# The first weight tile of a windowed matmul: two 1 MB halves on one hardware queue, or one half and two quarters spread over two queues

## The chip, the cores and the metric

The kernel runs on one core of a Trainium2 chip. The metric is the device time of one execution in microseconds (us).

## The reference

```python
B, S, D, W = 4, 4096, 4096, 64
for b in range(B):
    o = int(offsets[b])
    results.append(x[b, o:o+W] @ w)      # w is 4096 x 4096, fp32
```

Four windows of 64 rows each are multiplied by one matrix of 64 MB. Nearly all bytes that the kernel moves are `w`, and each is read once.

## The kernel before

The four windows fill two groups of 128 rows (`G = 2`). `w` is cut into 32 k tiles of 128 rows. GpSimd's queue, which can cast while it copies, loads them as fp16 in blocks of up to four k tiles (8 MB read). GpSimd's first packets come late, so the first k tile is loaded ahead of them, as fp32, by the hardware queue of the sync engine (SP), into a tile that is free until later (`acc[1]`), and the scalar engine (ACT) casts it:

```python
    w0_32 = acc[1]
    nc.sync.dma_start(out=w0_32[:, :NG], in_=w[0:P, :NG])          # NG = 2048: 128 rows of 8 KB
    nc.scalar.dma_start(out=off_t[:], in_=offsets[None, :])
    nc.sync.dma_start(out=w0_32[:, NG:], in_=w[0:P, NG:])
    nc.scalar.copy(out=w_one[0][:, :NG], in_=w0_32[:, :NG])
    nc.scalar.copy(out=w_one[0][:, NG:], in_=w0_32[:, NG:])
    ...
    nc.gpsimd.dma_start(out=w_one[1][:], in_=w[P : 2 * P, :])      # second k tile, cast on the way
    ...                                                            # x, at addresses read from off_t
    for k0, r in blocks[2:]:                                       # the weight blocks, 3 buffers
        ...
        nc.gpsimd.dma_start(out=t[:, base : base + r * N], in_=w[k0 * P : (k0 + r) * P, :].rearrange(...))
```

x is transposed by matmuls as soon as it has landed; then come the first two k tiles and the blocks.

Of the kernel before, what the change touches and what calls it, by code (L numbers as in the profile page):

```python
# [10 lines left out]
def kernel(  # L11
# [7 lines left out]
    nc = tc.nc  # L19
# [4 lines left out]
    _, N = w.shape  # L24
    WIN = out.shape[1]
    P = 128
    NT = 512
    NG = N // 2
# [32 lines left out]
    ctx.enter_context(tc.manual_schedule())  # L61

    w0_32 = acc[1]
    nc.sync.dma_start(out=w0_32[:, :NG], in_=w[0:P, :NG])
    nc.scalar.dma_start(out=off_t[:], in_=offsets[None, :])
    nc.sync.dma_start(out=w0_32[:, NG:], in_=w[0:P, NG:])
    nc.scalar.copy(out=w_one[0][:, :NG], in_=w0_32[:, :NG])  # L67
    nc.scalar.copy(out=w_one[0][:, NG:], in_=w0_32[:, NG:])  # L68
# [4 lines left out]
    for b in range(B):  # L73
# [9 lines left out]
            out=x16[g][m * WIN : (m + 1) * WIN, :],  # L83
            in_=x[b][bass.ds(o, WIN), :],
# [8 lines left out]
    for k0, r in blocks[2:]:  # L93
        if free < r:
# [5 lines left out]
            out=t[:, base : base + r * N],  # L100
            in_=w[k0 * P : (k0 + r) * P, :].rearrange("(p r) n -> p (r n)", r=r),
# [13 lines left out]
    for ng, st in zip(order, (steps, fine_steps)):  # L115
        for ki, n, c0, c1 in st:
            wd = c1 - c0
            nc.gpsimd.dma_start(  # L118
                out=t[:, pos : pos + n * wd].rearrange("p (t n) -> p t n", t=n),
                in_=w[ki * P : (ki + n) * P, ng * NG + c0 : ng * NG + c1].rearrange(  # L120
                    "(t p) n -> p t n", p=P
                ),
# [14 lines left out]
    for g in range(G):  # L137
        for t in range(4):
            for i in range(8):
                nc.tensor.matmul(  # L140
                    out=pairs[t][:, i * P : (i + 1) * P],
# [126 lines left out]
```

## Time and profile before

| | before |
|---|---|
| time, median of 6 runs | 182.14 us (181.95 to 182.30) |
| span of the profiled run | 180.1 us |
| busy share of PE / DVE / ACT | 71% / 46% / 9% |
| read from HBM, written | 71.3 MB, 4.2 MB |

The busy shares say little here: no compute engine is full, while the DMA engines are. The windows of four single microseconds of the kernel before. Columns: the stretch and its length, busy time of PE, PE's weight loads, DVE, ACT and POOL (with numbers of instructions), granted clock, mean busy share of the 16 DMA engines, GB/s written. The last two count a packet wholly in the microsecond in which it starts, so the share can exceed 1.

```profile
2.00:3.00 1.00, 0.00 (x0) 0.00 (x0) 0.00 (x0) 0.70 (x1) 0.55 (x3) 1.00 0.88 205
3.00:4.00 1.00, 0.00 (x0) 0.00 (x0) 0.00 (x0) 0.00 (x0) 0.46 (x1) 1.00 0.91 369
4.00:5.00 1.00, 0.00 (x0) 0.00 (x0) 0.00 (x0) 0.00 (x0) 0.59 (x2) 1.00 1.01 426
5.00:6.00 1.00, 0.00 (x0) 0.00 (x0) 0.00 (x0) 0.20 (x1) 0.53 (x2) 1.00 1.16 360
```

(From 5 us on part of the traffic is cast from 4 bytes to 2, so that the column of bytes written falls.)

### The profile page before, as it was taken

The page shows a single profiled execution, that of the slowest core. Times are in us where ns is not written, and L with a number is a line of the kernel's source. Part 1 is how long each engine was busy: PE and PEld are TensorE (multiplying, and loading weights), DVE is VectorE, ACT ScalarE, POOL GpSimd, SP SyncE. Part 2 cuts the span into 40 slices and gives each one's busy share as a digit, 9 for nine tenths or more (in the row PEclk, how much of TensorE's full clock was granted, in tenths as well). Part 3 has the DMA queues.
Part 4 walks back from the last instruction along what each step waited for, and adds up shares of the span by engine and source line. Part 5 has one row for each costly group of instructions (what it writes and reads, how often), then busy time and mean ns, then how long its engine had stood idle before and what let it go on. Part 6 is the DMA issues. An engine that isn't in the chain of part 4 may idle for free.

```text
span 180.1 us, 1403 instructions
## 1 busy us (share of the span) xinstructions
PE 128.2 (71%) x576; PEld 57.3 (32%) x576; DVE 82.2 (46%) x68; ACT 16.9 (9%) x15; POOL 12.7 (7%) x27
## 2 busy tenths in 40 slices
PE   0000789104999499938996599949999999999910
PEld 0000764001344134413442134414444444443400
DVE  0000566200276427642566036733778975407560
ACT  2422346200000000000000000000000004004000
POOL 4600000000000100010001000020007100000200
PEclk9999999855599969996999569987999999999995
DMA  5999979999998899999989999999999999999996
GB/s 187 313 260 213 286 160 211 236 233 226 233 233 175 182 233 233 236 218 233 204 175 218 233 233 220 222 193 202 229 206 215 198 211 213 214 214 207 338 412 241
DMA packets 4151, 40.97 MB, mean 227 GB/s; under 512 B 434, under 2 KB 434, under 8 KB 2226
## 3 DMA queue, kind: packets, MB, share of 16 engines
q0 software_dynamic: 3280, 36.70, 93.5%
q1 hardware_dynamic: 576, 3.15, 4.6%
q10 hardware_dynamic: 290, 1.05, 1.5%
q8 instruction: 4, 0.07, 0.1%
q14 instruction: 1, 0.01, 0.0%
HBM read 71.30 MB, written 4.19 MB: 419 GB/s over the span
## 4 chain that ended last, share of the span: by engine, by line
DMA 43%; PE 43%; issue 4%; DVE 2%; another core or an unknown queue 1%; POOLq 1%; DVEq 1%; POOL 1%
DMA wc<-in_w_dram 43%; PE banks L154 43%; DVE acc L164 2%; DVEq L263 1%; POOLq L75 1%; POOL xrow L82 0%; POOL identity masks.py:197 0%; POOLq L82 0%; POOL w L71 0%; POOLq masks.py:199 0%; DVEq L164 0%; POOLq L252 0%
## 5 line engine op out<-in xcount | busy, mean ns | idle before, releaser
L154 PE MATMUL banks<-wc,xT 128*128 128x512 f16 x480 | 115.8, 405 | 23.6 <-DMA wc<-in_w_dram 23.3
L164 DVE TENSOR_TENSOR acc<-acc,banks 128x1024 f32<-128x1024 f32 x56 | 67.9, 1221 | 69.0 <-PE banks L154 68.4
L154 PEld LDWEIGHTS <-xT 128*128 128x128 f16 x512 | 52.3, 103 | 93.9 <-DMA wc<-in_w_dram 26.4
L140 PE MATMUL banks<-identity,xrow 128*128 128x128 f16 x64 | 5.3, 261 | 19.9 <-DMA xrow<-in_x_dram 19.9
L209 ACT COPY tmp<-banks 128x1024 f32<-128x1024 f32 x4 | 3.9, 1016 | 128.2 <-PE banks L154 128.2
L149 DVE CAST xT<-banks 128x1024 f16<-128x1024 f32 x4 | 4.8, 1222 | 21.5 <-PE banks L140 21.5
L99 POOL DMA_DIRECT2D wc<-in_w_dram x8 | 4.3, 539 | 108.1 <-PE banks L154 108.1
L140 PEld LDWEIGHTS <-xrow 128*128 128x128 f16 x64 | 5.1, 127 | 20.0 <-issue 20.0
L154 PE MATMUL banks<-w,xT 128*128 128x512 f16 x32 | 7.1, 379 | 0.0
L182 DVE COPY acc<-banks 128x1024 f32<-128x1024 f32 x4 | 4.9, 1225 | 1.6 <-PE banks L154 1.6
L118 POOL DMA_DIRECT2D wc<-in_w_dram x6 | 3.9, 674 | 17.1 <-PE banks L154 17.1
L213 DVE TENSOR_TENSOR acc<-acc,tmp 128x1024 f32<-128x1024 f32 x4 | 4.7, 1218 | 0.0
L151 ACT CAST xT<-banks 128x1024 f16<-128x1024 f32 x4 | 4.0, 1014 | 7.9 <-PE banks L140 7.9
L184 ACT COPY acc<-banks 128x1024 f32<-128x1024 f32 x4 | 4.0, 1012 | 3.0 <-PE banks L154 3.0
L200 POOL DMA_DIRECT2D out_dram<-acc x2 | 1.1, 537 | 27.2 <-DVE acc L213 27.2
L68 ACT CAST w<-acc 128x2048 f16<-128x2048 f32 x1 | 1.9, 1898 | 4.8 <-DMA acc<-in_w_dram 4.8
L82 POOL DMA_DIRECT2D xrow<-in_x_dram x4 | 2.1, 524 | 2.1 <-issue 2.1
L67 ACT CAST w<-acc 128x2048 f16<-128x2048 f32 x1 | 1.9, 1898 | 3.1 <-DMA acc<-in_w_dram 3.1
L67 ACT ACT_TABLE_LOAD x1 | 1.3, 1283 | 1.4 <-PEq L252 1.4
L71 POOL DMA_DIRECT2D w<-in_w_dram x1 | 0.7, 660 | 0.8 <-POOLq L252 0.8
masks.py:199 POOL TENSOR_SCALAR_AFFINE_SELECT identity<-identity 128x128 f16<-128x128 f16 x1 | 0.3, 287 | 0.1
masks.py:197 POOL MEMSET identity<- 128x128 f16 x1 | 0.2, 223 | 0.0
(4 smaller groups left out, 0.4 us busy)
## 6 DMA issues: line engine op xcount, KB each, us to landing
wc<-in_w_dram POOLq DMA_DIRECT2D x5, 4096.0 KB, 42.1
wc<-in_w_dram POOLq DMA_DIRECT2D x4, 1024.0 KB, 24.5
wc<-in_w_dram POOLq DMA_DIRECT2D x1, 3072.0 KB, 37.1
acc<-in_w_dram SPq DMA_DIRECT2D x2, 1024.0 KB, 8.1
xrow<-in_x_dram POOLq DMA_DIRECT2D x4, 512.0 KB, 14.4
wc<-in_w_dram POOLq DMA_DIRECT2D x1, 2048.0 KB, 26.4
out_dram<-acc POOLq DMA_DIRECT2D x2, 1024.0 KB, 5.6
w<-in_w_dram POOLq DMA_DIRECT2D x1, 1024.0 KB, 11.8
```

What stands on the lines that cost most here:

```text
L67: nc.scalar.copy(out=w_one[0][:, :NG], in_=w0_32[:, :NG])
L99: nc.gpsimd.dma_start(out=t[:, base : base + r * N], in_=w[k0 * P : (k0 + r) * P, :].rearrange("(p r) n -> p (r n)", r=r),)
L118: nc.gpsimd.dma_start(out=t[:, pos : pos + n * wd].rearrange("p (t n) -> p t n", t=n), in_=w[ki * P : (ki + n) * P, ng * NG + c0 : ng * NG ...
L140: nc.tensor.matmul(out=pairs[t][:, i * P : (i + 1) * P], lhsT=x_cols(g, 8 * t + i), rhs=identity[:], start=True, stop=True,)
L149: nc.vector.tensor_copy(out=dst, in_=pairs[t][:])
L151: nc.scalar.copy(out=dst, in_=pairs[t][:])
L154: nc.tensor.matmul(out=banks(bank), lhsT=xT[g][:, kt * P : (kt + 1) * P], rhs=rhs, start=start, stop=stop,)
L164: nc.vector.tensor_add(out=dst, in0=dst, in1=banks(bank, n))
L182: nc.vector.tensor_copy(out=dst, in_=banks(b0, 2))
L184: nc.scalar.copy(out=dst, in_=banks(b0, 2))
L209: nc.scalar.copy(out=tmp[g][:], in_=banks(4 * g + 2, 2))
L213: nc.vector.tensor_add(out=dst, in0=dst, in1=tmp[g][:])
```

## The change

Its intent is to get the first half of the tile in sooner, by loading it as two quarters, one on each hardware queue:

```diff
     w0_32 = acc[1]
-    nc.sync.dma_start(out=w0_32[:, :NG], in_=w[0:P, :NG])
+    Q = N // 4
+    nc.sync.dma_start(out=w0_32[:, :Q], in_=w[0:P, :Q])
     nc.scalar.dma_start(out=off_t[:], in_=offsets[None, :])
+    nc.scalar.dma_start(out=w0_32[:, Q:NG], in_=w[0:P, Q:NG])
     nc.sync.dma_start(out=w0_32[:, NG:], in_=w[0:P, NG:])
```

## The prediction

> **What bounds the kernel now.** I read the page first, then the chain of waits in order of time, the matmuls' timeline, the start's timeline, and the windows of the first microseconds. The page's slices say which resource is full, and the chain says where it sets the end:
>
> ```profile
> PE   0000789104999499938996599949999999999910
> ACT  2422346200000000000000000000000004004000
> PEclk9999999855599969996999569987999999999995
> DMA  5999979999998899999989999999999999999996
> ...
> DMA wc<-in_w_dram 43%; PE banks L154 43%; DVE acc L164 2%; DVEq L263 1%; POOLq L75 1%; POOL xrow L82 0%; POOL identity masks.py:197 0%; POOLq L82 0%; POOL w L71 0%; POOLq masks.py:199 0%; DVEq L164 0%; POOLq L252 0%
> ```
>
> The reader is to see that the DMA engines are about full in nearly every slice from the second on, that the matrix engine is not, and that neither the first k tile's load (acc<-in_w_dram) nor its casts on ACT stand in the chain. The matmuls' timeline shows how the two resources divide the span:
>
> ```profile
> 43.07 16.75 PE L154 MATMUL banks<-wc,xT 128*128 128x512 f16 x64 [10.79 <-DMA wc<-in_w_dram]
> 62.34 15.66 PE L154 MATMUL banks<-wc,xT 128*128 128x512 f16 x64 [2.52 <-DMA wc<-in_w_dram]
> 81.76 15.67 PE L154 MATMUL banks<-wc,xT 128*128 128x512 f16 x64 [3.75 <-DMA wc<-in_w_dram]
> 101.14 16.73 PE L154 MATMUL banks<-wc,xT 128*128 128x512 f16 x64 [3.71 <-DMA wc<-in_w_dram]
> 120.44 49.93 PE L154 MATMUL banks<-wc,xT 128*128 128x512 f16 x218 [2.57 <-DMA wc<-in_w_dram]
> ```
>
> Blocks of 8 MB of weights arrive every 19.3 us ((120.44-43.07)/4), about 433 GB/s of reading; PE needs 15.7 to 16.8 us for each and waits 2.5 to 3.8 us. After 120.44 us it no longer waits for long: 218 matmuls in one piece, then the last additions and stores. So the end is "landing of the fifth block" plus a fixed PE and store tail, and the landing is the sum of all DMA work queued before it, as the engines never run dry. Only what adds to that sum, or removes idle time from it, can move the end. The start, which the change touches:
>
> ```profile
> 0.86 0.52 ACTq L65 DMA_DIRECT2D off_t<-in_offsets_dram  x1
> 0.87 0.38 SPq L64 DMA_DIRECT2D acc<-in_w_dram  x1
> 1.30 0.42 SPq L66 DMA_DIRECT2D acc<-in_w_dram  x1
> 1.39 0.66 POOL L71 DMA_DIRECT2D w<-in_w_dram  x1 [0.81 <-POOLq L252]
> 1.42 1.28 ACT L67 ACT_TABLE_LOAD   x1 [1.42 <-PEq L252]
> ...
> 5.80 1.90 ACT L67 CAST w<-acc 128x2048 f16<-128x2048 f32 x1 [3.10 <-DMA acc<-in_w_dram]
> ...
> 12.53 1.90 ACT L68 CAST w<-acc 128x2048 f16<-128x2048 f32 x1 [4.83 <-DMA acc<-in_w_dram]
> ...
> 18.31 3.40 PE L140 MATMUL banks<-identity,xrow 128*128 128x128 f16 x32 [18.31 <-DMA xrow<-in_x_dram]
> ...
> 23.29 1.95 PE L140 MATMUL banks<-identity,xrow 128*128 128x128 f16 x32 [1.58 <-DMA xrow<-in_x_dram]
> ...
> 25.21 5.12 PE L154 MATMUL banks<-w,xT 128*128 128x512 f16 x23
> ```
>
> The first k tile is cast by 14.43 us, and its first matmul runs at 25.21, after both transposes that wait for x. That is 10.8 us of slack. Even the x path has slack: the first two k tiles are done some 33 us into the span, and PE then idles 10.79 us until the first block lands at 43.03.
>
> **What the Trainium skill says.** "DMA: Bandwidth & Descriptors", section "Issuing engines are not separate DMA queues": DMAs of the sync, scalar and GpSimd engines run on the same 16 DMA engines and interleave, and issuing from several saves only issue time. The trace agrees: once the GpSimd queue's packets begin, about 5.25 us into the span, single-packet records of the sync queue (8 KB, 0.322 us) alternate with its own (0.624 us each), while the DMA share stays at 0.95 to 1.16. The same page, section "Queues, rings and completion order", says a DMA is split over k of at most 16 rings, and "Why a DMA increments its semaphore by 16 and not by 1" that a 128-partition tile takes all 16. So a quarter spreads as a half does, 8 rows per engine; the trace has 128 packets and 16 semaphore packets for each half. The latter section also says that only the full count means the data has landed, so a cast that reads both quarters must wait for two full counts. The present trace has no two-queue load to test that on.
>
> **The change part by part.** Bytes do not change: 2 MB of fp32 weights, no compute instruction added or removed.
>
> 1. *Packets.* Before: 128 rows of 8 KB for the first half, 8 per engine, 0.309 us each in the packet records once the stream runs: 8 x 0.309 = 2.47 us. After: 16 rows of 4 KB per engine. The only 4 KB packets on these two queues in the trace are the final stores, median 0.159 us; taking that for loads too is my estimate. 16 x 0.159 = 2.54 us. Added: +0.07 us of DMA time, and one more semaphore packet per engine at 0.009 us. Sum +0.08 us, in a stream that has no idle time, so on the path.
>
> 2. *Issue.* SP issues the same number of DMAs at the same times. ACT issues one more behind the offsets: from about 1.4 us, some 0.4 to 0.5 us long (the row of L66, and of L65). The offsets' DMA still goes first, so x is issued as before. Nothing here is on the path.
>
> 3. *Landing of the first half.* SP's first packets begin about 0.8 us after its issue (1.68 us); ACT's should begin near 2.2 us. Its 8 packets per engine then alternate with the sync queue's, which has 1 to 3 packets' lead and, its quarter done, puts 1 to 3 rows of 8 KB of the other half between. So the quarter on ACT ends 0.3 to 0.9 us (1 to 3 x 0.309) later than the half did: the first half lands a little **later**, not earlier.
>
> 4. *A new wait.* In the built instruction stream the ACT table load, which waited for no DMA, now carries the wait for ACT's quarter, ahead of the cast that waits for SP's. So its 1.28 us no longer hide under the transfer: the first cast should start near 5.80 + 0.3 to 0.9 + 1.3 = 7.4 to 8.0 us. It ends before 10 us, ahead of the second cast, whose half lands at about the same time as before (12 us, perhaps up to 1 us sooner, as fewer rows are left to alternate with GpSimd's). Of the 10.8 us of slack nothing near all is used: 0 us.
>
> 5. *Everything behind.* w1, x and the weight blocks are issued from the same GpSimd stream in the same order. With the same bytes ahead of them they land where they did, plus 0.08 us.
>
> Sum: 182.15 + 0.08 = 182.2 us.
>
> **Rivals.**
>
> *A faster ramp.* The first packet of each engine took 0.725 us (median of the first 16 records) and the second 0.361, against 0.309 later: some 0.45 us of the DMA engines' time is lost at the start. If a second queue, or smaller rows, filled that hole, the whole stream and with it the end would move forward by up to 0.4 us: 181.8. For it: the stream is on the path, so every tenth counts in full. Against it: ACT's packets come 0.5 us after SP's, when the hole is mostly over, and may have a slow first packet of their own. I give it about one chance in four to win 0.2 us or more.
>
> *4 KB rows cost more than I take.* At 0.20 us per row it would be 16 x 0.20 - 2.47 = +0.73 us: 182.9. Against it: the stores' 0.159 us, with no load at that size to confirm.
>
> *ACT becomes the wait.* If the late table load and cast held the first matmuls, one would see PE wait for ACT at 25 us. It would need ACT to lose over 10 us; and even then the 10.79 us of idle PE before 43.07 lies behind. No effect on the end.
>
> *The PE clock.* Half-clock stretches come and go (the PEclk row), and after 120.44 us PE has little slack. A 3.4 us stretch at half clock moved into that tail would cost about 1.7 us. Against it: the three runs of before agree within 0.16 us, and a shift of 0.1 us in the stream hardly changes PE's load.
>
> **Range and chances.** The centre is the sum, 182.2. The low side is the ramp in full plus scatter of some 0.2 us, 181.6; the high side is most of the costlier rows, 182.8. Two per cent are 3.6 us: no term above is half of that except the clock's, so within 2% gets 0.98 and the two sides 0.01 each.
>
> **What would show it right or wrong.** Right: two DMAs of 512 KB and one of 1024 KB for acc among the DMA issues; the first cast at 7.4 to 8.0 us with the table load just before it; the second cast at 11.5 to 12.8; transposes still from 18.3 and 23.3 us; blocks landing at 43.1, 62.4, ... 120.5; 4 KB load packets near 0.16 us. The ramp rival is shown if all block landings come 0.2 to 0.4 us sooner, the row rival if they come 0.3 us or more later. Wrong altogether if PE comes to wait for ACT before the first two k tiles, if x lands much later, or if the half-clock stretches fall otherwise after 120 us.

## The result, and the profile after

| | before | changed |
|---|---|---|
| median of 6 runs | 182.14 us | 182.98 us |
| lowest, highest | 181.95, 182.30 | 182.85, 183.08 |

The ratio is 1.0046 (95% interval 1.0033 to 1.0059). Ratios are computed as the mean time of one kernel's runs over that of the other's of the same rounds, so they are not quite the ratio of the medians quoted here. The change is a small loss of 0.84 us, clear of noise, within 2%, and above the predicted range, which ended at 182.8.

From the page of the changed kernel, the DMA row of the 40 slices and the chain of waits by line:

```profile
DMA  5999999999999999999999999989999999999996
...
DMA wc<-in_w_dram 43%; PE banks L156 42%; DVE acc L166 2%; DMA off_t<-in_offsets_dram 1%; POOLq L77 1%; DVEq L265 1%; POOL xrow L84 0%; POOLq L84 0%; DVEq L166 0%
```

As before, the stream is full from the second slice on and the chain alternates between weights and matmuls. New is an entry for `off_t`, the offsets: a suspect, tested below. The matmuls' timeline of the changed kernel:

```profile
44.13 16.83 PE L156 MATMUL banks<-wc,xT 128*128 128x512 f16 x64 [11.03 <-DMA wc<-in_w_dram]
63.46 15.67 PE L156 MATMUL banks<-wc,xT 128*128 128x512 f16 x64 [2.50 <-DMA wc<-in_w_dram]
...
121.43 51.27 PE L156 MATMUL banks<-wc,xT 128*128 128x512 f16 x224 [2.45 <-DMA wc<-in_w_dram]
```

The first block lands 44.13 - 43.07 = 1.06 us later, the fifth 121.43 - 120.44 = 0.99 us later, and the span is 0.9 us longer (181.0 against 180.1). So the whole loss is there before the first block is used, and nothing is added or won back in the next 77 us. The start of the changed kernel's timeline:

```profile
0.87 0.52 ACTq L66 DMA_DIRECT2D off_t<-in_offsets_dram  x1
0.87 0.38 SPq L65 DMA_DIRECT2D acc<-in_w_dram  x1
1.30 0.43 SPq L68 DMA_DIRECT2D acc<-in_w_dram  x1
...
1.42 0.38 ACTq L67 DMA_DIRECT2D acc<-in_w_dram  x1
...
13.04 1.28 ACT L69 ACT_TABLE_LOAD   x1 [13.04 <-DMA acc<-in_w_dram]
14.34 1.90 ACT L69 CAST w<-acc 128x2048 f16<-128x2048 f32 x1
16.14 1.89 ACT L70 CAST w<-acc 128x2048 f16<-128x2048 f32 x1
...
26.04 4.26 PE L156 MATMUL banks<-w,xT 128*128 128x512 f16 x19
```

The first half is complete at 13 us instead of 5.8, because the quarter on ACT's queue lands last of all. That is spectacular and costs nothing: the casts end at 18.03 us, and their first matmul runs at 26.04, behind the transposes of x. What does cost is in the windows of the changed kernel:

```profile
2.00:3.00 1.00, 0.00 (x0) 0.00 (x0) 0.00 (x0) 0.00 (x0) 0.56 (x3) 1.00 0.87 213
3.00:4.00 1.00, 0.00 (x0) 0.00 (x0) 0.00 (x0) 0.00 (x0) 0.00 (x0) 1.00 0.83 217
4.00:5.00 1.00, 0.00 (x0) 0.00 (x0) 0.00 (x0) 0.00 (x0) 0.53 (x1) 1.00 0.99 352
5.00:6.00 1.00, 0.00 (x0) 0.00 (x0) 0.00 (x0) 0.00 (x0) 0.53 (x1) 1.00 1.06 418
```

The second of these lines is the finding: 217 GB/s where the kernel before moves 369, at nearly the same busy share (0.83 against 0.91); spread over the packets' durations, 222 against 361. Full rate comes at 5 us, one microsecond later.

The trace also records single packets, and they were counted directly; these counts are used below. Up to 6 us into the span 1408 KB had been read before and 1165 KB after; up to 12 us, 3959 and 3717 KB. The missing 243 KB are 0.57 us at 427 GB/s. I call a packet slow when it took over 1.3 times the median of its size, and at least 60 ns more. Before, 21 of 256 rows of the first k tile were slow, most of them the first or second row of a DMA engine (up to 1.27 us instead of 0.309). After, 48 of the 128 rows of the quarter that opens the stream were slow (up to 1.06 us instead of 0.159), up to 4.6 us into the span; and from 2.0 to 2.75 us only 10.0 of the 16 engines had a packet in flight on average, against 14.5 before. (A single such count decides little: x3, a run below that loses nothing, has 11.1.)

Slow rows are only half of it. Per DMA engine, the delay splits into the time that the first k tile's packets took, and the time without a packet in flight between 1.88 and 5.2 us. The sum agrees within 0.04 us with how much later the mean engine reaches the first 8 MB block. One profile each, in us against the kernel before; the runs are explained below. Differences under 0.2 us mean little here: x3 sums to +0.16 and loses no time.

| run | packets | no packet in flight | later at the first block, mean engine |
|---|---|---|---|
| changed kernel | +0.31 | +0.28 | +0.56 |
| e1_rows_only | +0.08 | +0.33 | +0.39 |
| y1_one_queue_same_order | +0.43 | +0.21 | +0.61 |
| x2_quarters_last | +0.28 | 0.00 | +0.24 |
| e2_queue_only | +0.15 | -0.05 | +0.08 |
| y4_all_quarters | +0.59 | +0.27 | +0.86 |

Following the DMA engines to their first packets of the first 8 MB block, the mean start moved from 22.33 to 22.89 us and the slowest from 22.59 to 23.64. A block has landed only when all engines have delivered their rows, so the spread counts as well as the mean: the mean engine finishes the first block 0.56 us later (41.70 and 42.26 us), the last one 1.12 us later (42.69 and 43.81). That one engine trails the last but one by 0.80 us before and 0.87 after, so it alone sets the landing.

**Two levels.** Later runs showed that nearly every kernel here has a second level some 0.5 to 1.2 us above its first: of 11 runs of the kernel before in one batch, nine lay at 181.8 to 182.1 and two at 182.8. Profiled runs on the upper level show a lower granted clock in the stretch of back-to-back matmuls at the end. Here the same window for the changed kernel (lower level), for the run with whole rows (upper level) and for the changed kernel run again (upper level); the third figure from the right is the clock:

```profile
120.40:172.00 51.60, 50.31 (x222) 22.12 (x223) 30.20 (x26) 3.85 (x4) 4.99 (x8) 0.97 1.01 221
```

```profile
120.40:172.00 51.60, 50.86 (x221) 22.17 (x222) 29.92 (x25) 3.85 (x4) 4.99 (x8) 0.95 1.01 219
```

```profile
120.40:172.00 51.60, 50.13 (x216) 21.82 (x217) 28.87 (x25) 3.85 (x4) 5.00 (x8) 0.93 0.99 212
```

All 19 profiles follow this: 0.93 to 0.95 in the five on the upper level (and in y3, whose six runs spread too far to be sorted), 0.97 to 1.00 in the other thirteen; and where the last 224 matmuls run in one piece they take 52.1 to 52.4 us on the upper level and 51.2 to 51.3 on the lower. That is a correlation of the right size; no run changed the clock to test it. To keep the draw out of the comparisons I quote, besides the median and the ratio over all runs, the median of the runs on a kernel's lower level. The grouping is mine, and an intermediate run now and then could be sorted either way. The kernel before is at 182.0 to 182.1 in that reading in every later batch.

### The profile page after: what moved, and what is told of

Read it like the earlier page. It is cut to its first block, busy times and chain, and to the rows that moved or that the text cites. A ratio compares the mean times of both kernels' runs of the same rounds, so it can differ in the third digit from the quotient of the medians.

```text
span 181.0 us, 1405 instructions
## 1 busy us (share of the span) xinstructions
PE 128.6 (71%) x576; PEld 57.3 (32%) x576; DVE 82.2 (45%) x68; ACT 16.8 (9%) x15; POOL 12.7 (7%) x27
## 4 chain that ended last, share of the span: by engine, by line
DMA 45%; PE 42%; issue 4%; DVE 2%; another core or an unknown queue 1%; POOLq 1%; DVEq 1%; POOL 0%
DMA wc<-in_w_dram 43%; PE banks L156 42%; DVE acc L166 2%; DMA off_t<-in_offsets_dram 1%; POOLq L77 1%; DVEq L265 1%; POOL xrow L84 0%; POOLq L84 0%; DVEq L166 0%
## 6 DMA issues: line engine op xcount, KB each, us to landing
acc<-in_w_dram SPq DMA_DIRECT2D x1, 1024.0 KB, 10.8
w<-in_w_dram POOLq DMA_DIRECT2D x1, 1024.0 KB, 12.8
```

## The experiments

Three theories stood at first. ROWS: the short rows are to blame. QUEUE: the second hardware queue is. OFFSETS: the offsets' packet, at 2.61 us instead of 1.75 in the profiled run, delayed x.

| run | what opens the stream, and what follows | median, us | lower level (runs on it) | ratio to before |
|---|---|---|---|---|
| changed kernel | 4 KB quarter, half, quarter on ACT | 182.98 | 182.98 (6 of 6) | 1.0046 |
| e1_rows_only | quarter, quarter, half, all on SP | 182.64 | 182.62 (5 of 6) | 1.0035 |
| e2_queue_only | half on SP, half on ACT | 182.12 | 182.07 (5 of 6) | 1.0005 |
| e3_offsets_first | as changed, offsets first on SP | 182.52 | 182.52 (5 of 6) | 1.0029 |
| e4_whole_rows | one transfer, 16 KB rows | 182.49 | 182.04 (3 of 6) | 1.0011 |
| x1_after_again | as changed | 183.39 | 182.91 (3 of 6) | 1.0065 |
| x2_quarters_last | half, then the two quarters | 182.22 | 182.22 (6 of 6) | 1.0003 |
| x3_late_offsets | half, offsets, half on SP | 182.04 | 182.03 (5 of 6) | 1.0002 |
| x4_eighths | four 2 KB pieces, half | 184.46 | 184.46 (4 of 4) | 1.0127 |
| y1_one_queue_same_order | quarter, half, quarter on SP | 182.93 | 182.91 (5 of 6) | 1.0050 |
| y2_half_on_scalar | two quarters on SP, half on ACT | 183.53 | 182.75 (1 of 6) | 1.0071 |
| y4_all_quarters | four quarters on SP | 183.74 | 183.73 (5 of 6) | 1.0096 |
| z4_two_short_row_transfers | 1 MB transfers of 4 KB rows | 184.54 | 184.48 (3 of 5) | 1.0149 |
| z5_quarter_then_rest | quarter, then 12 KB rows | 182.83 | 182.75 (4 of 6) | 1.0052 |

All runs gave correct results. Four more runs (y3, z1, z2, z3) stand with their times in the section on the opening.

### Row length or second queue: e1_rows_only, e2_queue_only

```diff
-    nc.scalar.dma_start(out=w0_32[:, Q:NG], in_=w[0:P, Q:NG])
+    nc.sync.dma_start(out=w0_32[:, Q:NG], in_=w[0:P, Q:NG])
```

> Both quarters of 4 KB rows on the sync queue, then the other half; the scalar queue carries the offsets alone. Theory ROWS (4 KB rows make the start of the stream slower, whichever queue they are on): as slow as the changed kernel, 182.8 to 183.2 us. Theory QUEUE (the second hardware queue, with its late start and its mixing, delays some DMA engines): back at the kernel before, 182.0 to 182.3. Theory OFFSETS (the offsets' packet, 0.9 us later in the changed kernel, delays x and with it the end): follows the offsets' packet, 182.2 if it is back at 1.75 us, 183.0 if it is at 2.6 us.

```diff
 # from the kernel before
-    nc.sync.dma_start(out=w0_32[:, NG:], in_=w[0:P, NG:])
+    nc.scalar.dma_start(out=w0_32[:, NG:], in_=w[0:P, NG:])
```

> 8 KB rows throughout, as before, but the second half on the scalar queue behind the offsets. Theory ROWS: as the kernel before, 182.0 to 182.3 us. Theory QUEUE: slower by half of the loss or all of it, 182.6 to 183.0. Theory OFFSETS: as the kernel before if the offsets' packet comes at 1.75 us as there.

With the second queue alone the time is that of the kernel before (182.07, ratio 1.0005). With the cut alone it is 182.62, and the offsets' packet is at 1.75 us again, so that OFFSETS fails here too. The third and fourth microsecond show why. First the windows of e1_rows_only, then those of e2_queue_only:

```profile
2.00:3.00 1.00, 0.00 (x0) 0.00 (x0) 0.00 (x0) 0.00 (x0) 0.56 (x3) 1.00 0.81 209
3.00:4.00 1.00, 0.00 (x0) 0.00 (x0) 0.00 (x0) 0.00 (x0) 0.47 (x1) 1.00 0.85 238
```

```profile
2.00:3.00 1.00, 0.00 (x0) 0.00 (x0) 0.00 (x0) 1.00 (x1) 0.56 (x3) 1.00 0.87 172
3.00:4.00 1.00, 0.00 (x0) 0.00 (x0) 0.00 (x0) 0.10 (x1) 0.46 (x1) 1.00 0.91 344
```

With the 4 KB quarter at the opening the rate is 238 GB/s in the fourth microsecond, little above the 217 of the changed kernel; with the 8 KB half it rises to 344, second queue or not. So the cut carries most of the loss. But e1 loses 0.55 us and the changed kernel 0.85; 0.3 us were unexplained.

### The offsets: e3_offsets_first, x1_after_again, x3_late_offsets

```diff
 # e3, from the changed kernel
+    nc.sync.dma_start(out=off_t[:], in_=offsets[None, :])
     nc.sync.dma_start(out=w0_32[:, :Q], in_=w[0:P, :Q])
-    nc.scalar.dma_start(out=off_t[:], in_=offsets[None, :])
```

> The changed kernel, with the offsets' transfer issued first on the sync queue, ahead of that queue's quarter. Theory OFFSETS: the offsets' packet and the issue of x are back at their early times and the time falls to about 182.2 us. Theories ROWS and QUEUE: it stays at 182.8 to 183.2, although x is issued 0.6 us sooner.

x1_after_again is the changed kernel unaltered.

> The changed kernel unaltered, once more, to see whether its offsets' packet at 2.6 us and its slowest DMA engine (1.05 us behind the kernel before's at the first 8 MB block) are its own or a draw. Theory ROWS (4 KB rows cost 0.5 us wherever they open the stream; the rest of the 0.85 us is the late offsets' packet or scatter): the loss on the first block is 0.5 to 1.1 us, the time 182.5 to 183.0. Theory ORDER (the offsets' transfer behind a 4 KB quarter adds the other 0.3 us each time): offsets' packet again at 2.6 us and the time at 182.9 to 183.1.

```diff
 # x3, from the kernel before
-    nc.scalar.dma_start(out=off_t[:], in_=offsets[None, :])
+    nc.sync.dma_start(out=off_t[:], in_=offsets[None, :])
```

> The kernel before's two halves of 8 KB rows on the sync queue, with the offsets' transfer put between them on that queue, so that it lands later than in the changed kernel and x is issued later. Theory ROWS: no change, 182.0 to 182.3 us, as x waits behind the second k tile in its queue anyway. Theory OFFSETS: slower by 0.3 us or more, 182.4 to 183.2.

x3 put the offsets' packet at 4.96 us, far later than the changed kernel did, and the time is 182.03: no cost. x1 drew an early packet (1.76 us) and is as slow as ever, 182.91 on its lower level, with 58 slow 4 KB rows and the slowest DMA engine at 23.64 us, as in the first profile. So the late packet in the first profile was a draw, and the entry for `off_t` in the chain is a wait that costs nothing. OFFSETS and its variant ORDER are out. e3 alone would have misled: it gained 0.46 us, but it also put the two quarters one behind the other ahead of the half, as e1 does, and has e1's time.

### Position and dose: x2_quarters_last, x4_eighths, e4_whole_rows, y4_all_quarters

```diff
 # x2: the changed kernel's transfers and queues, the half first
+    nc.sync.dma_start(out=w0_32[:, NG:], in_=w[0:P, NG:])
     nc.scalar.dma_start(out=off_t[:], in_=offsets[None, :])
     nc.sync.dma_start(out=w0_32[:, :Q], in_=w[0:P, :Q])
     nc.scalar.dma_start(out=w0_32[:, Q:NG], in_=w[0:P, Q:NG])
-    nc.sync.dma_start(out=w0_32[:, NG:], in_=w[0:P, NG:])
```

> The same three transfers on the same queues, but the 8 KB half opens the stream and the two quarters follow. Theory COLD START (only the first 2 us of the stream are slow per packet, so that small rows cost there alone): as the kernel before, 182.0 to 182.3 us, with hardly any slow 4 KB packet. Rival (4 KB rows cost the same anywhere, or the third transfer does): 182.5 to 183.0.

```diff
 # x4: E = N // 8, offsets first, then
+    for i in range(4):
+        nc.sync.dma_start(out=w0_32[:, i * E : (i + 1) * E], in_=w[0:P, i * E : (i + 1) * E])
     nc.sync.dma_start(out=w0_32[:, NG:], in_=w[0:P, NG:])
```

> The dose doubled: the first half as four pieces of 2 KB rows, all on the sync queue, then the other half in 8 KB rows; offsets first. Theory COLD START: the first piece moves half as many bytes per slow packet, so the loss grows from the 0.5 us of rows-only to 0.7 to 1.3 us: 182.8 to 183.4. Theory that the loss is a fixed cost of a third transfer or a draw: 182.5 to 182.7.

```diff
 # e4: offsets, then
+    nc.sync.dma_start(out=w0_32[:, :], in_=w[0:P, :])
```

> The whole first k tile as one transfer of 128 rows of 16 KB on the sync queue: the row size changed the other way. Theory ROWS: at the kernel before or faster, 181.6 to 182.2 us, with less time lost per DMA engine before the first 8 MB block. Theories QUEUE and OFFSETS: the kernel before's time, 182.0 to 182.3.

```diff
 # y4: first quarter, offsets, then
+    for i in range(1, 4):
+        nc.sync.dma_start(out=w0_32[:, i * Q : (i + 1) * Q], in_=w[0:P, i * Q : (i + 1) * Q])
```

> All four quarters in 4 KB rows, one after the other on the sync queue. Theory COLD START (only the rows that open the stream cost): as rows-only, 182.5 to 182.7 us in the lower level. Theory that each 4 KB row costs alike, wherever it stands: twice the loss of rows-only, 183.0 to 183.2.

x2 is the cleanest run. The same three transfers, on the same two queues, cost about 0.15 us (ratio 1.0003, not clear of noise) instead of 0.85 when the half goes first; only 7 of its 256 rows of 4 KB are slow. Its windows of the same two microseconds are those of a good start:

```profile
2.00:3.00 1.00, 0.00 (x0) 0.00 (x0) 0.00 (x0) 0.00 (x0) 0.55 (x3) 1.00 0.86 188
3.00:4.00 1.00, 0.00 (x0) 0.00 (x0) 0.00 (x0) 0.00 (x0) 0.46 (x1) 1.00 0.87 328
```

The dose works in one direction only. Shorter rows cost more, and more than I expected: 2 KB rows lose 2.3 us where I had written 0.7 to 1.3. Longer rows (e4) win nothing; on the lower level they are at 182.04. And the opening is not all: y4 has e1's opening and the same 0.82 to 0.83 MB read by 5 us, but ends 1.1 us later than e1. Two parts of that can be read from the records. First, its engines reach the first 8 MB block 0.47 us later than e1's (0.86 against 0.39 above), all of it packet time, against the expectation of COLD START that later 4 KB rows are free. Of this, 0.18 us is their price beside GpSimd's packets: on SP's queue a 4 KB row takes 0.172 us there and an 8 KB row 0.322, so two short rows cost 0.022 us more than a long one, and y4 has eight such pairs per engine more than e1. Second, 0.42 us are lost after the last store and have nothing to do with rows. At its end SP checks a row of semaphores one after the other, and in y4 the wait for the last store comes first instead of near the end. SP's wait for the stores in e1, then in y4 (us in total, number of waits, the longest):

```profile
SPq L265 <- DMA out_dram<-acc: 4.0, 4, 1.2
```

```profile
SPq L265 <- DMA out_dram<-acc: 4.7, 1, 4.7
```

In y4 the whole wait falls on one instruction, and seven more, some 0.06 us each, run after it. From the last packet of the stores to the end of the span it is 1.70 us in y4, 1.71 in z1 and 1.64 in x4, and 1.26 to 1.29 in the other 16 profiles. These three kernels have the most transfers ahead of the stream; what orders the waits was not looked into. So about 0.4 us of the losses of y4, z1 and x4 come from the end of the program.

### The missing 0.3 us: y1_one_queue_same_order, y2_half_on_scalar, z5_quarter_then_rest

```diff
 # y1, from the changed kernel
+    nc.sync.dma_start(out=w0_32[:, NG:], in_=w[0:P, NG:])
+    nc.sync.dma_start(out=w0_32[:, Q:NG], in_=w[0:P, Q:NG])
-    nc.scalar.dma_start(out=w0_32[:, Q:NG], in_=w[0:P, Q:NG])
-    nc.sync.dma_start(out=w0_32[:, NG:], in_=w[0:P, NG:])
```

> Rows-only cost 0.5 us (182.6), the changed kernel costs 0.85 (182.9 in the lower of the two levels that every kernel shows). Here all three transfers are on the sync queue, in the order in which the changed kernel's packets started: first quarter, 8 KB half, second quarter. Theory SECOND QUEUE (the other 0.3 us comes from two hardware queues at once): 182.5 to 182.7 in the lower level. Theory ORDER OF SIZES (it comes from the half following the first quarter directly): 182.8 to 183.0.

```diff
 # y2, from the changed kernel: the second and third weight transfers change queues
+    nc.sync.dma_start(out=w0_32[:, Q:NG], in_=w[0:P, Q:NG])
+    nc.scalar.dma_start(out=w0_32[:, NG:], in_=w[0:P, NG:])
-    nc.scalar.dma_start(out=w0_32[:, Q:NG], in_=w[0:P, Q:NG])
-    nc.sync.dma_start(out=w0_32[:, NG:], in_=w[0:P, NG:])
```

> Both quarters on the sync queue, the 8 KB half on the scalar queue: two hardware queues as in the changed kernel, but the large rows on the other. Theory SECOND QUEUE: 182.8 to 183.0 us in the lower level. Theory ORDER OF SIZES: 182.5 to 182.7, if the second quarter's packets start before the half's; 182.9 if not.

```diff
 # z5: first quarter, offsets, then
+    nc.sync.dma_start(out=w0_32[:, Q:], in_=w[0:P, Q:])
```

> A first quarter of 4 KB rows, then all the rest as one transfer of 12 KB rows, both on the sync queue. Both theories: slower than before. SMALL OPENING TRANSFER and ORDER OF SIZES: as the changed kernel, 182.8 to 183.0 in the lower level, as large rows follow the quarter directly. If only the count of 4 KB rows mattered (half as many as in rows-only): 182.3.

y1 uses one queue only and has the changed kernel's whole loss: 182.91 on the lower level, ratio 1.0050. That settles that no second queue is needed for it. What y1 shares with the changed kernel, and e1 and e3 do not, is the half directly behind the first quarter: in the trace of the changed kernel the half's first row starts at 4.01 us, while ACT's quarter, issued 0.12 us after the half, starts only at 4.68. The fifth microsecond of y1 moves 340 GB/s (352 in the changed kernel, 393 in e1). That rate alone does not explain the 0.3 us, as z5 moves 442 in it and y2 406, and both lose 0.7. z5, with 12 KB rows behind the quarter, is at 182.75, between the two. y2 has one run on its lower level, and decides nothing by itself; its first block, at 43.80 us, lies between e1's 43.67 and y1's 43.99.

### Which property of the opening: y3, z3, z1, z2, z4

These runs asked what makes opening rows slow. Three of them (y3, z3, z4) have a confounder, and z1 has another at its end.

```diff
 # y3_long_rows_same_queues: first half in two blocks of 64 partitions, 8 KB rows (H = 64)
+    nc.sync.dma_start(out=w0_32[:H, :NG], in_=w[0:H, :NG])
+    nc.scalar.dma_start(out=w0_32[H:, :NG], in_=w[H:P, :NG])
 # z3_odd_even_rows: the same with even and odd partitions
+    nc.sync.dma_start(out=w0_32[0:P:2, :NG], in_=w[0:P:2, :NG])
+    nc.scalar.dma_start(out=w0_32[1:P:2, :NG], in_=w[1:P:2, :NG])
```

> The changed kernel's three transfers, sizes, queues and order, but the first half is cut by partitions (64 rows of 8 KB on each queue) instead of by columns: only the row length differs. Theory ROWS (short rows at the start of the stream are the whole cause): as the kernel before, 181.9 to 182.2 us in the lower level. Theory SECOND QUEUE or a cost of a third transfer: 182.3 to 182.9.

> The changed kernel's three transfers, sizes, queues and order; the first half is cut into even and odd partitions (64 rows of 8 KB each) instead of columns. Theory ROWS: as the kernel before, 181.9 to 182.2 us in the lower level. Theory that 64-partition transfers are slow whichever partitions they name: 183.8 or more, as in the run cut into two blocks. Theory that a third transfer or a second queue costs: 182.3 to 182.9.

Neither behaved like the kernel before. y3 has a median of 184.85 us (183.80 to 185.49), z3 of 182.92 (ratio 1.0047). Taken at their word, they refute ROWS in its strict form, that row length is the whole cause. But both started 0.3 us later (first packet at 2.18 us against 1.88), and y3's first issue took 0.54 us instead of 0.38. A cut by partitions brings a cost of its own, and these runs do not isolate row length. But the late start covers only 0.3 of the 0.8 us that z3 loses with 8 KB rows, so a rival stands: that an opening transfer of half the size (0.5 MB) is slow, whatever its rows.

```diff
 # z4: two transfers of 1 MB, each with two 4 KB pieces of every row (dst, row: views "p (h n) -> p h n", h = 4)
+    nc.sync.dma_start(out=dst[:, 0:4:2, :], in_=row[:, 0:4:2, :])
+    nc.sync.dma_start(out=dst[:, 1:4:2, :], in_=row[:, 1:4:2, :])
```

> Two transfers of 1 MB on the sync queue, as before, but each takes two 4 KB pieces of every row (first and third quarter, then second and fourth), so that all rows are 4 KB. Theory ROW LENGTH: at least the loss of rows-only, 182.6 us or more in the lower level, with 30 or more slow packets at the start. Theory SMALL OPENING TRANSFER: near the kernel before, 182.0 to 182.4 (some cost of 4 KB rows beside the GpSimd queue, as with the quarters last), with full rate reached at about 4.0 us.

z4 is far above what the theory of a small opening transfer allows: 184.48, with 119 slow rows and under 340 GB/s until at least 6 us into the span. So 1 MB in one transfer did not save short rows here. It too started late (2.29 us, issue 0.63 us), which can account for 0.4 of its 2.4 us.

```diff
 # z1_prelude_quarters: the changed kernel; z2_prelude_halves: the kernel before; both behind
+    nc.sync.dma_start(out=acc[0][:, :NG], in_=w[N // 2 : N // 2 + P, :NG])    # 1 MB, not used
```

> The changed kernel, with 1 MB of other weights in 8 KB rows (read into a tile that is overwritten later, not used) opening the stream ahead of it. The added bytes alone cost about 2.5 us at 427 GB/s: some 184.6 us. To be read against z2_prelude_halves. Theory COLD START (the stream's first 2 us are slow, whatever is read): the same time as z2 within 0.2 us, with few slow 4 KB packets. Theory FIRST TOUCH (the rows of the first k tile are slow when first read): slower than z2 by 0.6 to 0.9 us, with 30 or more slow 4 KB packets.

> The kernel before with the same 1 MB prelude: about 182.05 + 2.5 = 184.5 us in the lower level. Under COLD START its first half has no slow packets, under FIRST TOUCH again about 20.

The medians are 186.11 us (ratio 1.0233) and 185.53 us (1.0193), both more than the added bytes explain (1 MB at 427 GB/s is 2.5 us, and z2 lost 3.4). As to the question: behind the prelude only 7 rows of 4 KB were slow instead of 48 (z1), and no row of the first half (z2; its prelude has about 20), so slowness belongs to the opening of the stream and not to the first reading of these addresses. The quarters still cost 0.5 us more than the halves, between the two expectations; but 0.42 us of that is z1's longer end (1.71 us after the last store against 1.29), and what is left is near x2's 0.15, as COLD START had it.

**What is settled and what is not.** The loss comes from opening the stream with the 4 KB quarter: alone it costs 0.55 us (e1), with the half directly behind it 0.85 (y1), and with the half first about 0.15 (x2). The second queue and the offsets are cleared (e2, y1, x3, x1). Not settled: whether it is the short rows or the smaller opening transfer that counts (y3, z3 and z4, each with a confounder, speak for both), what inside the DMA path makes such an opening slow, why the order behind it adds 0.3 us, and some 0.3 us of y4's packet time. No variant beat the kernel before; e2, x3 and e4 match it.

## Why the prediction was wrong, point by point

- *What bounds the kernel*: right. The end followed the first block's landing almost to the tenth (1.06 us at the first block, 0.99 at the fifth, 0.9 in the span), with nothing absorbed on the way. Some readings were off without touching the sum: the last piece of matmuls, cut at 170 us in that view, is 224 of them in 51.23 us; the first two k tiles are done at 32.3 us; and the single-packet times are 0.2 us early (GpSimd's first packet is at 5.46 us, not 5.25, and SP's at 1.88, not 1.68).
- *Part 1, packets*: **the step that failed.** It put the cost of the cut at "+0.07 us of DMA time", by pricing sixteen 4 KB rows at a steady 0.159 us, "in a stream that has no idle time". The steady figure was right for one half of them: ACT's quarter has a median of 0.159 us and took 1.28 us per engine, as priced. But the first quarter does not run in the steady state. 48 of its 128 rows were slow, so it took 2.06 us per engine instead of 1.27, and an engine spent 0.28 us more than before without any packet. (The opening half before had cost 3.07 instead of 2.47, so only a part of the slow rows is new.) The term was 0.55 us for the cut alone (e1) and 0.85 with the half directly behind the quarter (x1, y1), instead of 0.08. That the opening rows are slow was in the trace of before (0.725 us for the first row instead of 0.309); I used it only for a possible gain.
- *Part 2, issue*: right. ACT's second issue ran from 1.42 us for 0.38 us, and SP's were unmoved. (In the first profile x was issued 0.6 us later, at 4.15 us instead of 3.54; in x1 it was at 3.53 again.)
- *Part 3, landing of the first half*: right in sign, wrong in mechanism and size. ACT's quarter was to begin near 2.2 us, alternate with SP's rows and end 0.3 to 0.9 us late. It began at 4.68, when 146 of SP's 256 rows had started, and was complete about 7 us late, as its rows then ran beside SP's half and GpSimd's packets. The same holds where SP's transfer was issued ahead of ACT's in other runs: ACT's first row came after 115 of SP's 128 rows in e2 (4.89 us), and after 150 of 256 in y2 and x2. The two hardware queues did not alternate from the start; why, no run shows.
- *Part 4, the new wait*: the mechanism was right, the table load waits for ACT's quarter, and it costs nothing. The cast was to start at 7.4 to 8.0 us and started at 14.34, the second at 11.5 to 12.8 and started at 16.14, by the error of part 3; the 10.8 us of slack held, with 8.0 us to spare (26.04 - 18.03).
- *Part 5, everything behind*: "they land where they did, plus 0.08 us". They landed 1 us later, by part 1.
- *Rivals*: the faster ramp went the other way. "4 KB rows cost more than I take" gave 182.9 and nearly hit the 182.98. That is luck in the number: its uniform 0.20 us per row did not occur, but very slow rows and idle engines at the start did; I argued it away with stores from the end of the kernel, where the stream is long in motion. The clock rival fits the upper level, 0.5 to 1.2 us, but fell on neither kernel in the deciding six runs.

## What to carry to other kernels

Price a transfer by where it stands: in the kernels here the rows that open the DMA stream were slower than those of the same size later (0.725 against 0.309 us for 8 KB), so open with a large transfer of long rows and put short ones behind (0.15 us lost instead of 0.85 here). When the stream is full to the end, a loss in its first 5 us reaches the end undiminished, while a wait of 7 us off that path costs nothing. Before blaming the part of a change that stands out in the profile (the late cast, the new entry in the chain), undo that part alone. And when a variant changes the number of transfers, compare the end of the program too (0.4 us in y4, z1 and x4).

## What the Trainium skill lacked or had wrong

- "DMA: Bandwidth & Descriptors", section "Specifications", gives a first-byte latency of about 0.6 us for the hardware path and 1 us for GpSimd's, without saying from when. Here the first packet of an idle SP queue came 1.02 us after its issue began (0.87 to 1.89 us) and 0.64 us after it ended, so the figure fits if it is counted from the end. It is no guide once other transfers are ahead: ACT's quarter came 3.26 us after its issue began (1.42 to 4.68) and GpSimd's first packet 4.07 us (1.39 to 5.46, kernel before).
- The same page, section "Rules for kernel authors", asks for 128 partitions and at least 1 MiB per DMA. The runs agree in direction: two 64-partition blocks have a median of 184.85 us and the 0.5 MB quarter one of 182.98, against 182.1. It does not say that the opening of the stream is the place where this counts: the same 0.5 MB quarters behind the half cost about 0.15 us (x2). Nor does it speak of rows: two 1 MB transfers of 4 KB rows lost 2.4 us (z4, of which 0.4 is a late start).
- No page that I read tells of a ramp. Here the stream ran at 205 GB/s in its first full microsecond and at 426 two microseconds later, and with a 4 KB quarter at its head one microsecond later still (windows of before and after).
- Nothing is wrong in the page's statement that several issuing engines gain no bandwidth, cited in the prediction: the second queue alone changed the time by a factor of 1.0005 (0.9984 to 1.0026).
